# Later norms at stage changes, layer 0's context first, and weight low parts on VectorE in a two-block transformer kernel

## The chip, the core and the metric

The kernel runs on one core of a Trainium2 chip. The metric is device time of one execution in microseconds (us). Engines: TensorE (PE in the profile; its weight loads are PEld), VectorE (DVE), ScalarE (ACT), GpSimd (POOL) and SyncE (SP), which here only issues DMAs.

## The reference

Two blocks of two layers each, on 512 tokens of width 1024, all in float32. The first block also carries 256 context tokens through its layer 0.

```python
for i in range(2):                                   # first block
    u_lat = modulate(rms_norm(h_lat, g_mix[i]), sh1, sc1)    # shifts and scales: silu(c) @ ada_w[i]
    u_ctx = modulate(rms_norm(h_ctx, g_mix[i]), csh1, csc1)
    # i = 0: neighbourhood attention (16 heads) over a 8x64 grid plus context; i = 1: sliding window
    h_lat = h_lat + ga1 * y_lat                      # y = attention @ wo; layer 0: h_ctx likewise
    h_lat = h_lat + ga2 * squared_relu_mlp(
        modulate(rms_norm(h_lat, g_mlp[i]), sh2, sc2), mlp_w1[i], mlp_w2[i])
for l in range(2):                                   # second block
    hn = rmsnorm(h, pre_g)
    y = even_mixer(hn) if l == 0 else odd_mixer(hn)  # diff. attention + mLSTM; gated spatial mixing
    h = h + rmsnorm(y, post_g)
```

Width of the MLPs: 4096. The output is `h` of the 512 tokens.

## The kernel before, in words

Activations lie transposed: features on the 128 partitions, eight tiles `hl[:, k, :]` of 512 tokens (`hc` for the 256 context tokens). Each large matmul is done in parts: a float32 operand is split into a high part (fp32r, a copy on ScalarE) and a low part (the float32 value minus that copy), by `split` (lines 125 to 128), and three products are summed: hi by hi, hi by lo, lo by hi. `lin` (line 145) does it for weights as the stationary operand, first all products with the weights' high part, then those with the low part (line 152); `tok` (line 154) for tokens as the stationary operand (line 160). Weights come by `load_w` (line 132): two DMAs of half a block into `wraw`, and four splits of 128x512. Their low parts are subtracted on GpSimd unless a call names another engine. `whi` and `wlo` have two buffers, `wraw` four.

An RMS norm is `rstd` (line 259): squares on ScalarE (line 266), seven adds on VectorE (line 268), a matmul with ones that sums over the partitions (line 270; line 272 for a late last square), `Ln` and `Exp` on ScalarE. `modulate` (line 277) follows for each of the eight tiles: a product on VectorE (line 280), then the split; for odd tiles the low part is on GpSimd, for even ones on VectorE (line 289, or 128).

Stages in order of time (us of the profile): adaLN and first norms (to 60), neighbourhood attention (to 460), its output projection `project_back(0)` (to 520), `mlp(0)` (to 1098), `sliding_window` (to 1340) and `project_back(1)` (to 1375), `mlp(1)` (to 1736), the even mixer with differential attention (to 2030), mLSTM (to 2285) and its output projection (to 2347), the odd mixer (to the end).

`project_back` does the first two blocks of columns for all tokens; the last two are done token group by token group, and after each group `done` is called, which is the norm of the next stage for that group. In layer 0 the groups are all 512 tokens, then the context; in layer 1 two halves of 256. `mlp` takes eight groups of hidden features; `up(g+1)` is emitted before `down(g)`. In `up(0)` each token group has its own matmuls; in the last `down` the tokens are in halves, then the context, and `done` is called after each. `update` (line 418) adds a product times its gate to the residual, on VectorE. During `mlp(0)` the adaLN products of layer 1 are made on VectorE by `ada_vector` (lines 229 and 231), some steps at each `between()` after a weight load. `project_out` is the output projection of the second block; with `room` it calls `done(c)` after each half, which there is the post norm and the next pre norm. In the odd mixer, `value_tile` makes values of 128 tokens, with Gelu on ScalarE after the last norm's `Exp` (`issue_after`).

The order of the source gives precedence: work emitted first goes first on an engine when it can, and a scheduler at build time sets the order of each engine's queue. [...]

## Time and profile before

| | us |
|---|---|
| median of 3 runs | 2733.99 |
| lowest and highest | 2729.48, 2734.04 |
| the profiled run, its own time | 2738.25 |
| its span in the profile | 2736.4 |
| TensorE busy in it | 2603.4 |

The page's slices show TensorE busy nine tenths and more in nearly all of the 40 slices. "Busy" of TensorE counts from the start of a matmul to its modelled end; successive matmuls overlap, so the pitch of a run of matmuls is read from its length over their count. [...] In a list of waits, the instruction named after the arrow is the one that ended the idle time.

### The profile page before, as it was taken

Reading aid. Unit: us, or ns where it says so; the run is one execution under the profiler, and the core shown is the slowest. Engines: PE = TensorE matmul, PEld = TensorE weight load, DVE = VectorE, ACT = ScalarE, POOL = GpSimd, SP = SyncE. Lnnn points to the kernel's source line nnn. Section 1 sums busy time; section 2 is a strip of 40 time slices with the busy share of each in tenths; the row PEclk is TensorE's granted clock in tenths of the full one; section 3 lists DMA queues with packets and bytes.
Section 4 is the critical chain, followed back from the end, with each engine's and each line's share of the span. In section 5 each row is a group of like instructions: output and inputs, shape, how many; then the busy total and the mean of one; then the engine's idle time right before and its main releaser. Section 6 shows DMA issues by size and latency. Waiting matters only on the chain. (4 is left out here: it accounts for less than half of the span.)

```text
span 2736.4 us, 40968 instructions
## 1 busy us (share of the span) xinstructions
PE 2603.4 (95%) x15876; PEld 2201.9 (80%) x15876; DVE 1405.6 (51%) x2908; ACT 1254.8 (46%) x2664; POOL 1087.3 (40%) x932
## 2 busy tenths in 40 slices
PE   6999998999999999899999999899999999899998
PEld 4877776788888889777888888877778888898887
DVE  4667667675666567688552222544553444502024
ACT  5655555422222223588543332466654554544342
POOL 3221313333332322533254544544435555435453
PEclk9999999999999999999999999999999999999999
DMA  7211324243333342210123333322222222322321
GB/s 246 61 55 56 107 63 153 66 135 100 114 117 118 92 124 62 74 32 19 45 88 97 93 100 100 81 62 62 67 66 78 78 83 72 97 80 91 95 87 62
DMA packets 217635, 237.94 MB, mean 87 GB/s; under 512 B 9824, under 2 KB 179296, under 8 KB 217440
## 3 DMA queue, kind: packets, MB, share of 16 engines
q1 hardware_dynamic: 210464, 229.15, 27.7%
q10 hardware_dynamic: 6976, 6.17, 0.7%
q8 instruction: 125, 2.05, 0.3%
q14 instruction: 70, 0.57, 0.1%
HBM read 233.18 MB, written 2.10 MB: 86 GB/s over the span
## 5 line engine op out<-in xcount | busy, mean ns | idle before, releaser
L128 POOL TENSOR_TENSOR wlo<-wraw,whi 128x512 fp32r<-128x512 f32 x628 | 836.4, 1361 | 887.3 <-ACT whi L127 847.3
L152 PE MATMUL mm<-uhl,whi 128*128 128x512 f32 (+1 forms) x1480 | 574.3, 391 | 3.6 <-ACT whi L127 2.6
L152 PE MATMUL mm<-ull,whi 128*128 128x512 f32 (+1 forms) x1480 | 569.9, 388 | 4.3 <-POOL ull L128 2.1
L127 ACT ACTIVATE whi<-wraw 128x512 fp32r<-128x512 f32 (+1 forms) x632 | 354.0, 619 | 445.2 <-issue 276.7
L152 PE MATMUL mm<-uhl,wlo 128*128 128x512 f32 (+1 forms) x1480 | 406.3, 386 | 0.0
L152 PEld LDWEIGHTS mm<-uhl,whi 128*128 128x128 f32 x1480 | 282.0, 191 | 62.8 <-ACT whi L127 6.1
L152 PEld LDWEIGHTS mm<-ull,whi 128*128 128x128 f32 x1480 | 282.2, 191 | 56.9 <-POOL ull L128 3.7
L152 PEld LDWEIGHTS mm<-uhl,wlo 128*128 128x128 f32 x1480 | 270.2, 190 | 54.1 <-issue 2.2
L418 DVE SCALAR_TENSOR_TENSOR hl<-mm,mod,hl 128x512 f32<-128x512 f32 (+1 forms) x156 | 105.2, 679 | 226.9 <-PE mm L152 226.9
L152 PE MATMUL mm<-h1h,whi 128*128 128x512 f32 (+1 forms) x576 | 208.4, 369 | 0.0
L152 PE MATMUL mm<-h1l,whi 128*128 128x512 f32 (+1 forms) x576 | 208.1, 369 | 0.0
L152 PE MATMUL mm<-h1h,wlo 128*128 128x512 f32 (+1 forms) x576 | 161.8, 368 | 0.0
L160 PE MATMUL mm<-whi,uhl 128*128 128x256 f32 x608 | 155.0, 290 | 1.0 <-DVE t L297 0.5
L160 PE MATMUL mm<-whi,ull 128*128 128x256 f32 x608 | 152.9, 287 | 0.0
L231 DVE SCALAR_TENSOR_TENSOR aacc<-araw,csil,aacc 128x512 f32<-128x512 f32 x196 | 148.5, 811 | 2.5 <-DMA araw<-ada_w 2.4
L304 POOL TENSOR_TENSOR t<-t,t 128x512 f32<-128x512 f32 (+1 forms) x46 | 49.1, 1067 | 231.5 <-ACT t L301 132.1
L479 DVE TENSOR_TENSOR t<-mm,t 128x512 f32<-128x512 f32 (+1 forms) x96 | 53.1, 574 | 153.2 <-ACT t L474 153.1
L474 ACT ACTIVATE t<-mm 128x512 f32<-128x512 f32 (+1 forms) x100 | 47.7, 507 | 177.8 <-PE mm L152 177.8
L152 PE MATMUL mm<-ulc,whi 128*128 128x256 f32 x448 | 124.6, 286 | 1.1 <-POOL ulc L128 1.1
L152 PE MATMUL mm<-uhc,whi 128*128 128x256 f32 x448 | 124.8, 287 | 0.0
L152 PEld LDWEIGHTS mm<-h1h,whi 128*128 128x128 f32 x576 | 108.6, 188 | 19.6 <-issue 1.0
L152 PEld LDWEIGHTS mm<-h1l,whi 128*128 128x128 f32 x576 | 108.6, 189 | 18.7
(381 smaller groups left out, 5445.2 us busy)
## 6 DMA issues: line engine op xcount, KB each, us to landing
wraw<-mlp_w SPq DMA_DIRECT2D x128, 512.0 KB, 3.8
wraw<-l_w_in SPq DMA_DIRECT2D x88, 512.0 KB, 3.7
araw<-ada_w SPq DMA_DIRECT2D x112, 256.0 KB, 3.0
wraw<-l_w_out SPq DMA_DIRECT2D x32, 512.0 KB, 3.5
wraw<-ada_w SPq DMA_DIRECT2D x24, 512.0 KB, 4.2
wraw<-l_w_in SPq DMA_DIRECT2D x48, 256.0 KB, 3.3
wraw<-na_wqkv SPq DMA_DIRECT2D x32, 256.0 KB, 3.8
wraw<-swa_wqkv SPq DMA_DIRECT2D x12, 512.0 KB, 3.6
```

Source lines behind the costliest of these rows:

```text
L127: nc.scalar.activation(out=hi, in_=src, func=AF.Copy)
L128: lo_eng.tensor_tensor(out=lo, in0=src, in1=hi.bitcast(F32), op=ALU.subtract)
L152: nc.tensor.matmul(out=o[0], lhsT=a[:, i, ms], rhs=o[j][:, i, :], start=(start and n_ == 0), stop=(stop and n_ == len(terms) - 1))
L160: nc.tensor.matmul(out=ps, lhsT=x[:, i, :], rhs=w[:, i, :], start=(n_ == 0), stop=(n_ == len(terms) - 1))
L231: nc.vector.scalar_tensor_tensor(out=acc[v], in0=raw, scalar=x, in1=acc[v], op0=ALU.mult, op1=ALU.add)
L304: nc.gpsimd.tensor_tensor(out=q, in0=q, in1=r, op=ALU.mult)
L418: nc.vector.scalar_tensor_tensor(out=o, in0=ps, scalar=mod[i][:, 8 * which + m, v:v + 1], in1=h, op0=ALU.mult, op1=ALU.add)
L474: nc.scalar.activation(out=a, in_=p, func=AF.Relu)
L479: nc.vector.tensor_tensor(out=q, in0=p, in1=a, op=ALU.mult)
```

## The change

- `pending` is a list of postponed norms, and `flush(n)` emits them. Where `done` was called, it is now put on the list. `flush` is called halfway through the next token group: in `project_back` after block 2 of the columns, in `up(0)` before the third tile, in the last `down` before the fifth, in the sliding window between a group's keys and values, in the even mixer after the first half's queries and keys. In `project_out` and the odd mixer the post norm and the pre norm are flushed one by one.
- In layer 0 the context is the first group of `project_back` and of `up(0)`, and the 512 tokens follow in two halves. In `up(0)` (both layers) both weight blocks are loaded first, and all four tiles of a group follow one another.
- The low part of a weight is subtracted on VectorE, except within the head loops of the two attentions (`scr["lo"]` is GpSimd there, and VectorE again for the last pair of heads of the neighbourhood attention).
- In the odd mixer the first half's values of the first four blocks are summed two tiles to a bank, before the Gelu of any of them.

```diff
...
     upool = ctx.enter_context(tc.tile_pool(name="upool", bufs=1))
-    scr = {}
+    scr = {"lo": nc.vector}
...
                 y = slice(s.start + x.start, s.start + x.stop)
-                split(hi[:, y, :], lo[:, y, :], raw[:, x], lo_eng or nc.gpsimd)
+                split(hi[:, y, :], lo[:, y, :], raw[:, x], lo_eng or scr["lo"])
         return hi, lo
...
+    pending = []
+    def flush(n=9):
+        for _ in range(min(n, len(pending))):
+            pending.pop(0)()
...
-        def segments(ul, uc, halves=False):
+        def segments(ul, uc, halves=False, ctx_first=False):
             lat = [(0, hlat, c, parts(ul, c)) for c in HALF] if halves else [(0, hlat, LAT, ul)]
-            return lat + ([(1, hctx, CTX, uc)] if uc is not None else [])
-        def project_back(i, w, x, halves, done, room=None, ws=()):
+            c = [(1, hctx, CTX, uc)] if uc is not None else []
+            return c + lat if ctx_first else lat + c
+        def project_back(i, w, x, done, room=None, ws=()):
             whole = segments(*x)
-            split_ = segments(*x, halves=halves)
+            split_ = segments(*x, halves=True, ctx_first=True)
             ws = [*ws, None, None, None, None]
...
                         update(i, 2, 2 * b + m, v, h(2 * b + m)[:, c], p)
-                done(v, h, c)
+                    if b == 2:
+                        flush()
+                pending.append(lambda v=v, h=h, c=c: done(v, h, c))
...
                     hid = hidden()
-                    for b in range(2):
+                    def load(b):
                         w = load_w([(0, 256, w1[:, 512 * g + 256 * b:512 * g + 256 * b + 256])], KD, 256)
                         between()
-                        sg = segments(*x, halves=halves and g == 0)
-                        groups = [[s] for s in sg] if g == 0 else [sg]
-                        for grp in groups:
-                            for m in range(2):
-                                j = 2 * b + m
-                                o = [(mm_tile()[:, :c.stop - c.start], xx) for _, _, c, xx in grp]
-                                lin([(p, *xx) for p, xx in o], w, slice(128 * m, 128 * m + 128))
-                                for (p, _), (v, _, c, _) in zip(o, grp):
-                                    act(p, hid[v][0][:, j, c], hid[v][1][:, j, c], i == 0 and g == 7 and v == 0)
+                        return w
+                    def tile_of(w, j, grp):
+                        o = [(mm_tile()[:, :c.stop - c.start], xx) for _, _, c, xx in grp]
+                        lin([(p, *xx) for p, xx in o], w, slice(128 * (j % 2), 128 * (j % 2) + 128))
+                        for (p, _), (v, _, c, _) in zip(o, grp):
+                            act(p, hid[v][0][:, j, c], hid[v][1][:, j, c], i == 0 and g == 7 and v == 0)
+                    if g == 0:
+                        ws = [load(b) for b in range(2)]
+                        for s in segments(*x, halves=True, ctx_first=True):
+                            for j in range(4):
+                                if j == 2:
+                                    flush()
+                                tile_of(ws[j // 2], j, [s])
+                    else:
+                        for b in range(2):
+                            w = load(b)
+                            for j in (2 * b, 2 * b + 1):
+                                tile_of(w, j, segments(*x))
                     return hid
...
                         for m in range(8):
+                            if last and m == 4:
+                                flush()
                             o = [(mm_tile()[:, :c.stop - c.start], xx) for _, _, c, xx in grp]
...
                             for v, h, c, _ in grp:
-                                done(v, h, c)
+                                pending.append(lambda v=v, h=h, c=c: done(v, h, c))
...
                 banks(mm="01", AD="2", NS="7", S="34", PT="5", ST="6")
+                scr["lo"] = nc.gpsimd
                 for hp in range(8):
...
                     if hp == 7:
+                        scr["lo"] = nc.vector
                         oh = (u_lat(), u_ctx())
...
-                project_back(0, A["na_wo"], oh, False, norm_after(0, "mlp", u), room, ws)
+                project_back(0, A["na_wo"], oh, norm_after(0, "mlp", u), room, ws)
             return u
+            if 1 not in u:
+                u[1] = u_ctx()
             ul, uc = u[0], u[1]
...
                         stack_k(kh[m], s, t)
+                    flush()
                     for t in range(n // 128):
...
                     split(oh[0][:, t, :], oh[1][:, t, :], pv, nc.vector)
+                scr["lo"] = nc.vector
                 banks(mm="0124", NS="7")
                 u = {}
-                project_back(1, A["swa_wo"], (oh, None), True, norm_after(1, "mlp", u))
+                project_back(1, A["swa_wo"], (oh, None), norm_after(1, "mlp", u))
             return u
...
                     block_out(b, c)
-                done(c)
+                    if b % 2 == 0:
+                        flush(1)
+                pending.extend(done(c))
             return
...
                 qk_proj(0, w0, HALF[x:x + 1])
+                flush()
                 v_proj(0, range(2 * x, 2 * x + 2))
...
         def done(c):
-            post_norm(yacc, vec("post0"), c)
-            norm(0, hlat, c)
+            return [lambda: post_norm(yacc, vec("post0"), c), lambda: norm(0, hlat, c)]
...
-        def value_tile(b, wv, t):
-            ps = mm_tile()[:, :256]
+        def value_mm(ps, wv, t):
             tok(ps, wv, parts(u, slice(128 * t, 128 * t + 128)))
+        def value_out(ps, b, t):
             o = vt[:, t, 256 * b:256 * b + 256]
+        def value_tile(b, wv, t):
+            ps = mm_tile()[:, :256]
+            value_mm(ps, wv, t)
+            value_out(ps, b, t)
...
         wv += [value_w(2 + j, (y[:, :, 0:256], y[:, :, 256:512]), nc.vector) for j, y in enumerate(y_tiles())]
-        with tc.issue_after(last_exp.ins):
+        early = []
+        for b in range(4):
+            ps = mm_tile()
+            for t in range(2):
+                value_mm(ps[:, 256 * t:256 * t + 256], wv[b], t)
+            early.append(ps)
+            if b % 2 == 0:
+                flush(1)
+        with tc.issue_after(scr["rstd"].ins):
             for b in range(4):
                 for t in range(2):
-                    value_tile(b, wv[b], t)
+                    value_out(early[b][:, 256 * t:256 * t + 256], b, t)
         for b in range(4):
...
```

## Rows read from the trace of the kernel before

**Rows 1.** The page, part 1: busy us (share of the span) xinstructions by engine
```profile
PE 2603.4 (95%) x15876; PEld 2201.9 (80%) x15876; DVE 1405.6 (51%) x2908; ACT 1254.8 (46%) x2664; POOL 1087.3 (40%) x932
```
**Rows 2.** TensorE's waits, whole span: who waited for whom, us in total, times, longest us
```profile
PE NS L270 <- DVE acc L268: 38.3, 10, 16.5
...
PE PT L1043 <- DVE p L1040: 8.6, 8, 2.0
PE NS L270 <- DVE pr L1007: 7.1, 1, 7.1
...
PE CU L1188 <- DVE kw L1186: 4.9, 3, 1.7
...
PE mm L152 <- DVE yl L128: 2.2, 1, 2.2
...
PE mm L160 <- POOL wlo L128: 1.2, 2, 0.7
```
**Rows 3.** Windows: stretch, length; busy of PE, PEld, DVE, ACT, POOL; PEclk; DMA share, GB/s
```profile
507.00:560.00 53.00, 43.23 (x249) 36.31 (x248) 47.24 (x67) 26.72 (x54) 22.37 (x16) 0.90 0.32 100
560.00:1060.00 500.00, 497.66 (x2993) 429.66 (x2992) 306.76 (x463) 119.78 (x239) 155.59 (x112) 1.00 0.37 112
1060.00:1121.00 61.00, 54.86 (x429) 52.33 (x428) 44.56 (x88) 34.78 (x83) 28.48 (x32) 0.97 0.18 57
...
1345.00:1392.00 47.00, 41.06 (x291) 38.55 (x290) 29.89 (x50) 23.78 (x57) 22.99 (x21) 0.96 0.30 87
...
1711.00:1752.00 41.00, 33.17 (x243) 32.03 (x242) 30.27 (x50) 18.68 (x46) 21.82 (x22) 0.88 0.31 84
...
2300.00:2374.00 74.00, 65.78 (x503) 64.38 (x502) 54.46 (x97) 32.91 (x85) 29.95 (x28) 0.93 0.27 84
```
**Rows 4.** Windows again, over ten stretches of low clock: one, and the sum
```profile
1741.00:1745.30 4.30, 0.00 (x0) 0.00 (x0) 4.20 (x3) 1.15 (x2) 3.44 (x3) 0.50 0.57 148
...
sum 37.60, PE 29.54 PEld 27.14 DVE 26.62 ACT 18.94 POOL 13.42; mean PE 2.95 PEld 2.71 DVE 2.66 ACT 1.89 POOL 1.34
```
**Rows 5.** Timelines, three stretches: start us, us, engine line op xcount [idle before <-releaser]
```profile
533.15 0.41 DVE L268 TENSOR_TENSOR acc<-acc,t 128x256 f32<-128x256 f32 x1
...
534.61 1.22 PE L270 MATMUL NS<-acc,ones 128*128 128x256 f32 x2 [5.15 <-DVE acc L268]
...
1725.18 0.70 PE L270 MATMUL NS<-acc,ones 128*128 128x256 f32 x2 [0.48 <-DVE acc L268]
...
1740.74 3.70 POOL L128 TENSOR_TENSOR wlo<-wraw,whi 128x512 fp32r<-128x512 f32 x3
1740.87 4.38 DVE L268 TENSOR_TENSOR acc<-acc,t 128x256 f32<-128x256 f32 x2
1745.31 1.22 PE L270 MATMUL NS<-acc,ones 128*128 128x256 f32 x2 [7.09 <-DVE pr L1007]
1745.97 0.78 PE L152 MATMUL mm<-uhl,wlo 128*128 128x256 f32 x1
```
**Rows 6.** The chain that ended last: start us, us, what (256 columns, then 512)
```profile
2364.26 79.54 PE mm L160 x666
2443.80 21.79 PE mm L152 x96
```
**Rows 7.** Timeline of VectorE after 534.61: last low part of that norm
```profile
542.23 0.47 DVE L289 SCALAR_TENSOR_TENSOR ulc<-t,mod,uhc 128x256 fp32r<-128x256 f32 x1
```
**Rows 8.** Groups of instructions: busy us, mean ns; or duration ns min/median/max
```profile
L128 POOL TENSOR_TENSOR wlo<-wraw,whi 128x512 fp32r<-128x512 f32 x624 | 833.6, 1365 | 884.3 <-ACT whi L127 847.3 <-PE mm L152 17.3 <-issue 10.9
L128 POOL TENSOR_TENSOR wlo<-wraw,whi x628: 727/1295/1868, 54.2 to 2703.8; 128x512 fp32r<-128x512 f32 x156, 128x256 fp32r<-128x256 f32 x1
L128 DVE TENSOR_TENSOR wlo<-wraw,whi x4: 684/686/693, 37.5 to 40.1; 128x512 fp32r<-128x512 f32 x4
L418 DVE SCALAR_TENSOR_TENSOR hl<-mm,mod,hl 128x256 f32<-128x256 f32 x40 | 18.5, 477 | 8.3 <-PE mm L152 8.3
```
**Rows 9.** Line 1227 on VectorE: duration ns min/median/max, first and last start
```profile
L1227 DVE SCALAR_TENSOR_TENSOR nctionType.Sigmoid<-nctionType.Sigmoid,vecs,t x8: 804/1702/1759, 2142.9 to 2290.8; 128x512 f32<-128x512 f32 x8
```

More of the change, by code (lines that the diff above doesn't have):

```diff
@@ L463, in mlp @@
         def mlp(i, with_ctx, u, done, between=lambda: None):
-            halves = not with_ctx
             x = (u[0], u[1] if with_ctx else None)
@@ L820, in sliding_window @@
                 banks(mm="0", NS="7", SL="12", SC="3", PT="45", ST="6")
+                scr["lo"] = nc.gpsimd
                 for t in range(8):
@@ L1250, in even, with odd @@
         return nu[0]
-    def odd(bp, yp, u, last_exp):
+    def odd(bp, yp, u):
         wi = A["l1_w_in"]
@@ L1345 @@
                 with tc.tile_pool(name="odd", bufs=1) as bp, tc.tile_pool(name="oddy", bufs=1) as yp:
-                    odd(bp, yp, u, scr["rstd"])
+                    odd(bp, yp, u)
     if stop < 5:
```

## The prediction

> **What bounds the kernel now.** I read the page's busy times first: TensorE is busy 95% of the span, the others about half or less [rows 1]. So the time is TensorE's work, plus its idle time, plus what it loses at the lower clock. Next comes the list of TensorE's waits [rows 2]. The largest is line 270, the ones-matmul that sums the squares of an RMS norm over the partitions, waiting for VectorE's adds (line 268): 38.3 us, and 7.1 us more put down to `pr`, a VectorE instruction just behind those adds. Of these 45.4 us the longest, 16.5, lies at the start of the kernel, which the change doesn't touch. The other 28.9 us (a short one at the very end among them) lie at five stage changes: neighbourhood attention to MLP 0, MLP 0 to sliding window, sliding window to MLP 1, MLP 1 to the even mixer, even to odd mixer.
>
> The table of windows [rows 3] gives length and TensorE's busy time at these five: 53-43.23, 61-54.86, 47-41.06, 41-33.17 and 74-65.78, together 37.9 us idle, of which 28.9 are the waits above and 9.0 are others. The granted clock is below 1 in each; in the 500 us of MLP 0 between them it is 1.00, with 2.3 us idle. [...]
>
> Why do the waits occur? The matmul at 1745.31 stood still for 7.09 us, and what follows it is the next stage's first tile (line 152, `uhl`): all of TensorE's later work queued behind one norm [rows 5]. What it waited for is VectorE's adds, and these are stretched: one 128x256 add takes 0.41 us alone, but two of them take 4.38 us while GpSimd runs three weight subtractions (3.70 us, line 128) in the same place. So at a stage change VectorE stands still while GpSimd subtracts, and TensorE stands still for VectorE.
>
> **The change part by part.** *Norms later.* A norm's instructions are now emitted after half of the next token group. Half a group of 256 tokens is 48 matmuls; 666 of that width took 79.54 us [rows 6], 0.119 us each, so 5.7 us. The two longest of the waits were 7.09 and 5.15 us [rows 5]: 5.7 us of other matmuls in front covers all but 1.4 us of the longer. I count 28.9-1.4 = 27.5 us gained. Where a gap remains the clock can still fall: of the 14.8 us I leave 4, about a quarter; 10.8 gained.
>
> The price: the next stage's input comes later. From a norm's matmul at 534.61 to the last of its low parts, 542.23+0.47, is 8.1 us [rows 5, 7]. Where the normed half is the very next thing read (MLP 1, the even and the odd mixer), 5.7 us of matmuls are left when its norm's matmul is issued, and 16 matmuls of 0.119 us (1.9 us) of the next tile go by before the last part is needed: 7.6 against 8.1. That is no margin. VectorE's load says the same. In the 23 us (192 matmuls) in which both halves of a norm must pass there are eight updates of 0.477 us, seven adds of 0.41, twelve instructions of 0.47 for the modulation, eight of about 0.41 for four tiles' activations, and now eight weight subtractions of 0.686 [rows 5, 7, 8]: 3.8+2.9+5.6+3.3+5.5 = 21.1 us. A new wait there lies between nothing and the old 7; I take 2 us at each of the three, 6 in sum, near the case just computed. At the other two changes the context's group lies between, 11.4 us more, and I take none, though at the first VectorE was busy 47.24 of 53 us [rows 3], with the adaLN products of line 231 in the same queue.
>
> *Context first, tokens in halves* (layer 0's output projection and first MLP group). 96+96 matmuls of 512 columns become twice as many of 256. 96 of 512 took 21.79 us, 0.227 each [rows 6]; two of 256 take 0.239. 192 x 0.012 = 2.4 us lost, on TensorE and so on the path. The vector work cut in two (products, adds, low parts) adds some 4 us on VectorE beside it, hidden as long as VectorE is ahead there; if it isn't, it is 4 us.
>
> *Low parts on VectorE.* Ten loads inside the neighbourhood loop and three in the sliding window's stay on GpSimd; of the others some 147 loads of four subtractions, 588 in all, move. GpSimd loses 588 x 1.365 = 803 us, VectorE gains 588 x 0.686 = 403 us [rows 8] and goes from 51% of the span to some 61%, the stretching gone. GpSimd's time was hardly on the path itself: TensorE waited 1.2 us for it [rows 2]. In MLP 0, the heaviest long stretch, VectorE goes from 307 to at most 307+128 x 0.686 = 395 of 500 us [rows 3]. So the subtractions cost nothing as long as they aren't queued behind a late instruction. At the changes they replace the stretch by work of a like size (three are 2.1 us, against 4.38-0.82 = 3.6 us of stretch), so I count nothing there. The gain lies in the mLSTM and in differential attention. Line 1227 takes 1.70 us as a rule and 0.80 at best, twice in a row [rows 9], and three state updates wait 4.9 us behind such pairs [rows 2]; I take 4. The wait of 2.2 us for the last head's low part, behind line 1227 and GpSimd's queue: 3, with some low clock that follows it, between 0 and 4. The 8.6 us of line 1043 wait for VectorE's scaled probabilities [rows 2]: 3, between 0 and 8.6, because VectorE now has subtractions in the same place. Together 10 us.
>
> [...]
>
> *Value tiles of the odd mixer* are summed two to a bank before the norm's last exponential. No matmul is added; it lets the flushes stand between them and is counted in the 27.5.
>
> **The sum.** 27.5+10.8-6-2.4+10 = 39.9 us off the profiled span of 2736.4, 2696.5. The profiled run took 2738.25, 1.85 more than its span and 4.3 above the median of the three runs, 2733.99. On the median's scale: 2733.99-39.9 = 2694.
>
> **The rivals.** First, *the wait moves instead of going.* Late norms make the next stage's first matmuls wait in all five places, 4 us each, and the clock falls as before: 27.5-20+10-2.4 = 15.1 gained, 2719. For it: 7.6 against 8.1 above, and VectorE nearly full at the first change. Against: a norm of the same trace in the middle of a group, at 1725.18, cost 0.48 us [rows 5].
>
> Second, *the queue's order doesn't follow the source*, and the norms stand where they stood, or VectorE's new subtractions eat all that the stretching cost. Then only 10-2.4 remain: 2726. For it: one norm matmul in the trace (1745.31) stands inside a tile of the next stage and not where the source has it, so the order in a queue is not the source's.
>
> Third, *slower: low parts late.* A subtraction queued on VectorE behind an update that itself waits for TensorE comes late, and TensorE waits for the weights just split. One subtraction late per load is 147 x 0.686 = 101 us. It outweighs the 39.9 when it befalls two loads in five; at one in two the time is 2694+51 = 2745. For it: VectorE's queue is full of instructions that wait for TensorE, the updates of line 418 above all. Against: a load has two buffers, and GpSimd, at twice the time per subtraction, was late by 1.2 us in total. [...]
>
> Fourth, *all of it*: no new waits, the clock never down, half of the other 9.0 us gone, and nearly all of line 1043's: 6+4+4.5+5.5 = 20 more, 2674.
>
> **How the numbers follow.** Forecast 0.52; wait moved 0.20; order unchanged 0.12; low parts late 0.08; all of it 0.08. About 0.2% (5.5 us) is what a measurement of this kernel can tell from no change. Faster: 0.52+0.20+0.08 and a third of the second rival, 0.84; within 0.2%: the rest of that, 0.08; slower 0.08. Range: from 2671, just under the fourth case, to 2722, where the first rival ends with 3 us for GpSimd's delays.
>
> **What would show it.** Right: line 270's waits at the five changes fall from 28.9 us to a few, with few stretches below full clock; GpSimd's busy time is near 285 us; no 128x256 add takes 1 us or more; 192 more matmuls run on line 152. The first rival shows as waits of lines 152 and 160 for `uhl` or `ull` right after a change. The second shows as line 270 with its old waits. The third shows as line 152 waiting for `wlo` from VectorE all through the MLPs. The prediction is wrong if line 270 no longer waits and TensorE's idle time stays.

## The result, and the profile after

The changed kernel takes 2689.72 us (median of 5 runs, 2686.89 to 2692.43), 0.9844 of the kernel before (95% interval 0.983 to 0.9859): 42.6 us less. The kernel before, run beside it, has a median of 2732.59 us over 5 runs. The profiled run took 2692.43 us, its span is 2690.3.

The first lines are of the page (busy us, share, instructions), then of the list of TensorE's waits (us in total, times, longest), of the groups of instructions (busy us, mean ns), and of the adds' durations (min/median/max in ns). All are of the changed kernel but the last line, which shows the same adds in the kernel before. The changed kernel's lines 129, 153, 161, 269, 271, 300, 426, 1079 and 1224 are 128, 152, 160, 268, 270, 299, 418, 1043 and 1188 of before.

```profile
PE 2596.4 (97%) x16070; PEld 2207.2 (82%) x16070; DVE 1622.2 (60%) x3527; ACT 1252.6 (47%) x2691; POOL 316.7 (12%) x348
```
```profile
PE NS L271 <- DVE acc L269: 22.9, 8, 15.0
PE NS L300 <- ACT t L297: 12.1, 9, 3.6
...
PE mm L161 <- ACT yh L128: 2.0, 1, 2.0
...
PE mm L161 <- ACT whi L128: 1.2, 1, 1.2
...
PE mm L153 <- DVE hl L426: 1.0, 1, 1.0
```
```profile
L129 DVE TENSOR_TENSOR wlo<-wraw,whi 128x512 fp32r<-128x512 f32 x576 | 383.9, 707 | 376.2 <-ACT whi L128 239.0 <-PE mm L153 79.6 <-PE mm L161 56.5
...
L129 POOL TENSOR_TENSOR wlo<-wraw,whi 128x512 fp32r<-128x512 f32 x52 | 71.6, 1400 | 53.9 <-ACT whi L128 41.3 <-PE mm L153 12.0 <-DVE nm L314 0.5
```
```profile
L269 DVE TENSOR_TENSOR acc<-acc,t x122: 407/425/962, 9.3 to 2677.4; 128x256 f32<-128x256 f32 x115, 128x512 f32<-128x512 f32 x7
```
```profile
L268 DVE TENSOR_TENSOR acc<-acc,t x115: 405/426/3851, 9.0 to 2723.5; 128x256 f32<-128x256 f32 x101, 128x512 f32<-128x512 f32 x14
```

Apart from the 15.0 us at the start, 7.9 us are left of line 271's waits, against 28.9 [rows 2]. The longest add falls from 3851 ns to 962. Line 1079's waits for probabilities and line 1224's for `kw` [rows 2] are no longer on the list. TensorE's idle time falls from 133 to 94 us, and 192 more matmuls run on line 153 (9912 against 9720). So the signs that the prediction asked for are there, two of them in part: GpSimd is busy 316.7 us where 285 were expected, and 20.4 us at the lower clock (a granted clock of 0.50, where 1.00 is the full one) are left at the changes (37.6 in [rows 4]). The signs don't tell which part of the change did it, and the experiments give another answer than the sum did.

The table is worked out from the traces. Each kernel's span is cut at the same instructions: the first and last transposes of each attention loop, the first and last matmuls that read an MLP's hidden low and high parts, the mLSTM's numerators, the odd mixer's first mixing matmul. Lengths in us; "five changes" are the stretches between one stage's loop and the next (longer than the windows of [rows 3]). "Late norms alone" has the new token order too; of the last two columns the first has the old token order and the second the new one. Each column is one trace; the start, where the third last column and "changed" run the same source, differs by 1.9 us between them, so a difference of that size in one stage says little.

| stage | before | changed | low parts alone | late norms alone | changed, prompt norms | prompt, more on VectorE | late, more on VectorE |
|---|---|---|---|---|---|---|---|
| start and neighbourhood loop | 459.0 | 450.4 | 450.5 | 455.9 | 448.5 | 440.5 | 441.2 |
| five changes | 564.3 | 544.5 | 525.7 | 566.5 | 528.1 | 513.3 | 531.6 |
| both MLPs | 799.8 | 797.6 | 797.1 | 800.6 | 797.7 | 795.3 | 796.4 |
| sliding-window loop | 162.3 | 164.9 | 163.5 | 162.0 | 163.5 | 162.8 | 161.4 |
| differential attention | 229.9 | 219.3 | 220.4 | 229.7 | 220.4 | 220.2 | 220.1 |
| to the mLSTM, and mLSTM | 250.0 | 242.4 | 242.4 | 249.8 | 242.3 | 242.4 | 242.4 |
| rest of the odd mixer | 271.0 | 271.0 | 271.0 | 271.3 | 271.0 | 271.0 | 271.0 |

At the five changes the changed kernel gained 19.8 us, where the sum had 29.9 (27.5+10.8-6-2.4). Elsewhere it gained 26.3, where the sum had 10.

### The profile page after: what moved, and what is told of

Its sections match the earlier page's. It is cut to its first block, busy times and chain, and to the rows that moved or that the text cites. A ratio compares the mean times of both kernels' runs of the same rounds, so it can differ in the third digit from the quotient of the medians.

```text
span 2690.3 us, 41389 instructions
## 1 busy us (share of the span) xinstructions
PE 2596.4 (97%) x16070; PEld 2207.2 (82%) x16070; DVE 1622.2 (60%) x3527; ACT 1252.6 (47%) x2691; POOL 316.7 (12%) x348
## 4 chain that ended last, share of the span: by engine, by line
PE 81%; DVE 10%; ACT 7%; issue 1%; DMA 1%; POOL 0%; SPq 0%; DVEq 0%; POOLq 0%; ACTq 0%
PE mm L153 60%; PE mm L161 7%; DVE t L281 1%; PE ST L701 1%; PE PT L680 1%; PE ST L864 1%; PE PT L847 1%; PE NS L300 1%; PE S L347 1%; DVE wlo L129 1%; ACT qx L327 1%; PE PO L1083 1%; ACT qx L333 1%; PE S L348 1%; PE AD L183 1%
## 5 line engine op out<-in xcount | busy, mean ns | idle before, releaser
L129 DVE TENSOR_TENSOR wlo<-wraw,whi 128x512 fp32r<-128x512 f32 (+1 forms) x580 | 385.5, 705 | 379.0 <-ACT whi L128 239.0
L153 PEld LDWEIGHTS mm<-uhl,whi 128*128 128x128 f32 x1528 | 288.2, 189 | 61.4 <-DVE t L298 4.4
L153 PEld LDWEIGHTS mm<-ull,whi 128*128 128x128 f32 x1528 | 288.5, 189 | 57.2 <-POOL ull L129 5.3
L129 POOL TENSOR_TENSOR ull<-t,uhl 128x256 fp32r<-128x256 f32 (+1 forms) x44 | 41.3, 944 | 1028.6 <-ACT uhl L128 1028.3
L232 DVE SCALAR_TENSOR_TENSOR aacc<-araw,csil,aacc 128x512 f32<-128x512 f32 x196 | 136.2, 751 | 0.4 <-DMA araw<-ada_w 0.4
L161 PEld LDWEIGHTS mm<-whi,uhl 128*128 128x128 f32 x608 | 116.8, 192 | 4.4 <-ACT whi L128 1.6
```

What stands on the lines that cost most here:

```text
L129: lo_eng.tensor_tensor(out=lo, in0=src, in1=hi.bitcast(F32), op=ALU.subtract)
L153: nc.tensor.matmul(out=o[0], lhsT=a[:, i, ms], rhs=o[j][:, i, :], start=(start and n_ == 0), stop=(stop and n_ == len(terms) - 1))
L161: nc.tensor.matmul(out=ps, lhsT=x[:, i, :], rhs=w[:, i, :], start=(n_ == 0), stop=(n_ == len(terms) - 1))
L232: nc.vector.scalar_tensor_tensor(out=acc[v], in0=raw, scalar=x, in1=acc[v], op0=ALU.mult, op1=ALU.add)
```

## The experiments

The first four split the change and test the stretch; four more say where it sits; the last four carry it further. Every ratio is to the kernel before, with its 95% interval.

**Low parts alone** (e1_low_parts_only).

```diff
 (kernel before)
-    scr = {}
+    scr = {"lo": nc.vector}      # nc.gpsimd inside the two attention loops
...
-                split(hi[:, y, :], lo[:, y, :], raw[:, x], lo_eng or nc.gpsimd)
+                split(hi[:, y, :], lo[:, y, :], raw[:, x], lo_eng or scr["lo"])
```

> The kernel before, with one edit: the weights' low parts are subtracted on VectorE instead of GpSimd, but for the loads inside the two attention loops, as in the changed kernel. Norms and token order stay as before. Theory A (two gains of like size): TensorE's interior waits go, since VectorE is no longer held up by GpSimd's subtractions: differential attention about 9 us shorter, mLSTM about 6, start and neighbourhood about 5, and at the five changes the norm's adds are no longer stretched, so line 270's 28.9 us shrink to about 20; the norm's own length stays there. About 20 to 28 us below the kernel before (0.7 to 1.0%). Rival B (all of it is the stretch of the adds): the waits of line 270 go with the stretch alone, about 40 us below. Rival C (the later norms do it all, the prediction's own weighting): 10 us below, the mLSTM and line 1043 only.

Measured: 2672.8 us, ratio 0.978 (0.9767 to 0.9794), 60 us below the kernel before, and 17 below the changed kernel. Its list of TensorE's waits, and line 268's durations:

```profile
PE NS L270 <- DVE acc L268: 22.3, 9, 15.0
PE NS L299 <- ACT t L296: 9.3, 10, 1.7
```
```profile
L268 DVE TENSOR_TENSOR acc<-acc,t x115: 405/424/957, 9.3 to 2657.7; 128x256 f32<-128x256 f32 x101, 128x512 f32<-128x512 f32 x14
```

In the source norms stand where they stood, and yet line 270 waits 7.3 us outside the start instead of 28.9; the five changes are 38.6 us shorter. Theory A's 20 to 28 and rival C's 10 fall. Rival B has the mechanism (the waits were the stretch of the adds) and too small a number, 40; the interior gains come on top. A rival that no run separates: the build sets TensorE's queue anew, and in it the norm's matmul stands 13, 10, 25 and 12 places later at the last four changes. At 0.119 us a matmul [rows 6] that is some 7 us of cover, an estimate. At the first change the matmul has the same place in both queues, and its wait still falls from 5.15 to 0.97 us.

**Late norms alone** (e2_norms_only).

```diff
 (changed kernel)
-    scr = {"lo": nc.vector}
+    scr = {"lo": nc.gpsimd}      # and so wherever it is set later
```

> The changed kernel with the weights' low parts back on GpSimd everywhere; norms half a group later, context first and tokens in halves as in the changed kernel. Theory A: the five changes keep most of their gain, since 5.7 us of matmuls stand in front of each norm, but the stretched adds and the later low parts eat some of it: 15 to 22 us below the kernel before. Rival B: next to nothing below it (within 5 us), since the norm is still held up by GpSimd's subtractions. Rival C: about 30 us below it, as the prediction's sum has it without the low parts.

Measured: 2736.84 us, ratio 1.0011 (1.0002 to 1.002): 0.5 to 5.5 us slower than the kernel before. Rival B holds, rival C (the prediction's weighting) is out. Its waits, first over the span, then from 1725 to 1790 us (MLP 1 to the even mixer) and from 1370 to 1430 (to MLP 1), and the durations of its adds:

```profile
PE NS L271 <- DVE acc L269: 27.9, 8, 15.7
...
PE PT L1079 <- DVE p L1076: 7.5, 8, 2.0
...
PE mm L238 <- issue: 5.3, 1, 5.3
...
PE CU L1224 <- DVE kw L1222: 4.9, 3, 1.6
```
```profile
PE mm L161 <- ACT whi L128: 4.1, 1, 4.1
PE NS L1044 <- DVE pr L1042: 2.6, 1, 2.6
```
```profile
PE mm L153 <- POOL ull L129: 2.8, 5, 1.2
```
```profile
L269 DVE TENSOR_TENSOR acc<-acc,t x122: 407/426/4371, 9.0 to 2722.7; 128x256 f32<-128x256 f32 x115, 128x512 f32<-128x512 f32 x7
```

The adds are as stretched as before (4371 ns at most). The delay did cover norms: line 271 waits 12.2 us outside the start, against 28.9. But TensorE's idle time at the five changes, added up from the traces, is 41.1 us against 44.0: of the 16.7 us covered, 13.8 came back. Among it are waits of the next stage's matmuls for high parts of weights queued behind the norm on ScalarE (4.1, none there before), for the norm's own low parts (2.8, 0.3 before), and of an adaLN product (5.3, 3.3 before). Most of the wait moved instead of going.

**Layer 0's tokens whole and in the old order** (e3_whole_tokens).

```diff
 (changed kernel)
-            split_ = segments(*x, halves=True, ctx_first=True)
+            split_ = segments(*x, halves=x[1] is None)
...
-                        for s in segments(*x, halves=True, ctx_first=True):
+                        for s in segments(*x, halves=not with_ctx):
```

> The changed kernel with layer 0's token order undone: in its output projection and in the first group of its MLP the 512 latent tokens go in one piece and before the context; norms stay late, low parts stay on VectorE. Theory A (192 matmuls at 0.012 us, and a stage in which VectorE has more, smaller instructions): 2.4 us less of matmuls, 192 matmuls fewer, but a wait of up to 5 us where the MLP's first tile reads all 512 tokens right after their norm: from 2 us shorter to 3 us longer than the changed kernel. Rival: the split tokens are what makes the first change cheap, and without them its 10 us of waits and low clock come back: 8 us longer or more.

Measured: 2691.63 us, ratio 0.9847 (0.9834 to 0.986), not to be told from the changed kernel, inside theory A's range. In its first change TensorE is busy 1.5 us less and idle 4.1 us more than in the changed kernel: the waits for the norm and for the normed input (from 450 to 600 us) eat what the wider matmuls save.

```profile
PE NS L271 <- DVE acc L269: 2.6, 1, 2.6
PE mm L153 <- ACT uhc L289: 2.2, 1, 2.2
PE mm L153 <- POOL ull L129: 2.0, 3, 1.3
```

**Spare subtractions on GpSimd** (e4_idle_copies). They compute nothing that is used.

```diff
 (changed kernel, after each subtraction that moved)
+                if (lo_eng or scr["lo"]) is nc.vector:
+                    h = hi[:, y, :].bitcast(F32)
+                    nc.gpsimd.tensor_tensor(out=junk[...], in0=h, in1=h, op=ALU.subtract)
```

> The changed kernel, and on GpSimd, for each subtraction that moved to VectorE, one subtraction of the same size whose result nobody reads (high part minus itself into a spare tile). Nothing waits for GpSimd that didn't before, apart from the spare work standing in its queue; the computation is the same. Theory A (VectorE is held up by GpSimd's reading and writing of SBUF): VectorE's instructions are stretched again, 100 to 150 us in sum over the span, and of the 43.6 us gained 15 to 30 are given back. Rival D (what counted was that the low part came late from a slow engine, 1.365 us against 0.686): the stretch may return, yet the time stays within 5 us of the changed kernel.

Measured: 2780.57 us, ratio 1.0172 (1.0158 to 1.0186): 91 us above the changed kernel, 47 above the kernel before. GpSimd is busy 1082.2 us, as before (1087.3, [rows 1]), and no instruction reads these results. TensorE, VectorE and ScalarE execute the same instructions as in the changed kernel, in the same order but for a few places, so queue order has no part in the 91 us. The groups of instructions (busy us, mean ns), then one group of the changed kernel, whose line 426 is line 430 here, then two of the waits with spare subtractions (line 275 is line 271 of the changed kernel):

```profile
L148 POOL TENSOR_TENSOR junk<-whi 128x512 f32<-128x512 f32 x576 | 741.7, 1288 | 926.5 <-ACT whi L129 890.8 <-DVE rl L845 3.4
...
L130 DVE TENSOR_TENSOR wlo<-wraw,whi 128x512 fp32r<-128x512 f32 x576 | 625.8, 1126 | 256.0 <-ACT whi L129 194.1 <-PE mm L157 60.8 <-issue 0.8
...
L130 DVE TENSOR_TENSOR h1l<-t,h1h 128x512 fp32r<-128x512 f32 x56 | 46.3, 826 | 12.8 <-ACT h1h L129 12.4
...
L430 DVE SCALAR_TENSOR_TENSOR hl<-mm,mod,hl 128x512 f32<-128x512 f32 x112 | 82.4, 746 | 117.8 <-PE mm L157 117.5
```
```profile
L426 DVE SCALAR_TENSOR_TENSOR hl<-mm,mod,hl 128x512 f32<-128x512 f32 x112 | 83.9, 750 | 171.5 <-PE mm L153 171.2
```
```profile
PE NS L275 <- DVE acc L273: 35.8, 10, 15.3
...
PE mm L165 <- ACT whi L129: 4.8, 1, 4.8
```

The subtraction on VectorE goes from 707 to 1126 ns, 241 us in sum: theory A's direction, with three times the upper end of its price. The moved subtractions, which follow the same high parts as the spare ones, take most of the stretch. Line 275 waits 20.5 us outside the start instead of 7.9, though the adds read no low part of a weight. Rival D, which wanted the time unchanged, falls; but since the low parts were late here too (1126 ns), the run doesn't separate stretch from lateness for the loads. Nor does it hold that nothing waits for the spare work: ScalarE's next high part waits 18 times, 223.2 us in all, until GpSimd has read `whi`. What reaches TensorE of this is little: its waits for `whi` and `wlo` are 9.2 us here and 3.0 in the changed kernel.

**Prompt norms in the changed kernel** (e6_prompt_norms).

```diff
 (changed kernel, the first pair of lines twice)
-                pending.append(lambda v=v, h=h, c=c: done(v, h, c))
+                done(v, h, c)
...
-                pending.extend(done(c))
+                for f in done(c):
+                    f()
```

> The changed kernel with one part undone: each norm is emitted as soon as its tokens are finished, as in the kernel before. Context first, tokens in halves, the two-to-a-bank value tiles and the low parts on VectorE stay. Known so far: low parts alone 2673, the changed kernel 2690. Theory E (the delay itself costs: norms that come half a group later leave their input late for the next stage's first tile, and the split tokens cost some 4.4 us of matmuls): 2675 to 2681, that is the low parts alone plus the split tokens. Rival F (the split and reordered tokens, or the value tiles, cost all 17 us): 2687 to 2692, as the changed kernel.

Measured: 2674.67 us, ratio 0.9788 (0.9774 to 0.9801). Just under the lower end of theory E. The delay costs 15 us (0.9844 against 0.9788). All else that came with it, split tokens, context first and value tiles, is 2 us above the low parts alone, within the intervals. At the first change by itself, where the split tokens are, it is 6.5 us (143.3 against 136.8, one trace each), of which 3.4 go to 6.8 us at the lower clock, 0.50 (the granted clock of the whole run is 0.996, with the low parts alone 0.998).

**Low parts only beside the changes** (e5_low_parts_at_changes): 41 of some 147 loads.

```diff
 (low parts alone)
-    scr = {"lo": nc.vector}
+    scr = {"lo": nc.gpsimd}
...
+                    scr["lo"] = nc.vector if g < 2 else nc.gpsimd            # MLP, up
+                    scr["lo"] = nc.vector if g == 0 or g > 5 else nc.gpsimd  # MLP, down
+            scr["lo"] = nc.gpsimd   # from differential attention on, nc.vector from the last projection to the odd mixer's sixth load
```

> The kernel before, with VectorE subtracting the low parts only of the some 41 loads that run next to the five stage changes (output projections, the first two and last groups of each MLP, the first loads of sliding window, even and odd mixer); all other loads stay on GpSimd, norms stay where they were. Theory G (the waits at the changes were VectorE held up by GpSimd's subtractions in the same microseconds): the five changes gain as with all low parts moved, 33 to 39 us, and differential attention, the mLSTM and the start gain nothing: 2694 to 2702. Rival H (it is the relief over the whole kernel, a backlog of VectorE that the MLPs build up): well under half of it, 2715 or more.

Measured: 2690.82 us, ratio 0.9845 (0.9832 to 0.9858). Theory G, a little beyond its range: 42 of the 60 us come from these loads. The five changes take 527.0 us (525.7 with all low parts moved), differential attention 230.9, as before. Theory G missed the start and neighbourhood loop, which it had at no gain: 450.9 us, 8.1 shorter, 5.2 of it in the last two pairs of heads, beside which the first of the 41 loads run. The interior waits stand as they stood:

```profile
PE PT L1049 <- DVE p L1046: 8.6, 8, 2.0
...
PE CU L1195 <- DVE kw L1193: 4.9, 3, 1.6
```

**The loads inside the attention loops too** (e7_all_weights).

```diff
 (low parts alone, twice)
-                scr["lo"] = nc.gpsimd
+                scr["lo"] = nc.vector
```

> Low parts on VectorE as in the kernel with them alone (2673), now for the 13 loads inside the two attention loops too: 52 subtractions more on VectorE (36 us more work, some 18 us less stretch), GpSimd 71 us less. Theory I (a VectorE that isn't held up has room): 0 to 6 us shorter. Rival J (in these loops VectorE's chain of softmax steps is on the path, and a subtraction in front of it costs its 0.69 us): 5 to 20 us longer, with the waits of the transposes for `p` up.

Measured: 2658.83 us, ratio 0.9732 (0.9718 to 0.9745), 13 us below the low parts alone; more than theory I had, and rival J's waits don't come. Start and neighbourhood take 439.6 us instead of 450.5. Line 651, one SBUF operand scaled by a column, in the kernel before and here:

```profile
L651 DVE TENSOR_SCALAR p<-p,rl x64: 471/486/1522, 88.8 to 451.8; 128x512 f32<-128x512 f32 x64
```
```profile
L651 DVE TENSOR_SCALAR p<-p,rl x64: 470/482/733, 83.3 to 434.0; 128x512 f32<-128x512 f32 x64
```

**The norms' odd low parts too** (e8_norm_parts).

```diff
 (low parts alone)
-            split(uh, ul, t, nc.gpsimd if k % 2 else nc.vector)
+            split(uh, ul, t, nc.vector)
...
-                split(uh, ul, t, nc.gpsimd)
+                split(uh, ul, t, nc.vector)
```

> Low parts on VectorE as in the kernel with them alone (2673), and the norms' odd low parts as well, 52 subtractions of 128x256 or 128x512 that GpSimd still does (50 us there). Theory K (GpSimd's last work in a norm still holds VectorE up, 15 to 18 us of stretch): 1 to 5 us shorter. Rival L (inside a norm VectorE is the longer queue, and each odd part adds 0.41 us to it): 2 to 8 us longer, as waits of the next stage's first tile for `ull` from VectorE.

Measured: 2657.74 us, ratio 0.9721 (0.9708 to 0.9734), 16 us below the low parts alone, three times theory K's upper end. Here splitting a norm's work over two engines was slower than one engine doing all: the waits for GpSimd's `ull` and `ulc` are gone and line 270 waits 4.8 us outside the start, nearly all on the way to the odd mixer and at the end. How much of this is VectorE relieved and how much order isn't shown: six of the norms' matmuls, line 270's, stand 7 to 25 places later in TensorE's queue than with the low parts alone, 79 in all (some 10 us at 0.119 us for 256 columns and 0.227 for 512, an estimate).

**Both** (e9_weights_and_norms), **and the same with late norms** (e10_late_norms_free): the two edits above, on the low parts alone and on the changed kernel.

> The kernel before with all weights' low parts and the norms' odd low parts on VectorE; norms at their old place. The two steps, one by one, brought 2673 to 2659 and to 2658. Theory R (they remove the stretch at different places, the attention loops and the five changes): the two gains add, 2641 to 2648. Rival S (VectorE, at some 61%, takes no more): 2653 or more.

> The changed kernel (late norms, context first, tokens in halves) with all weights' low parts and the norms' odd low parts on VectorE. Compared with the same at prompt norms, which runs beside it. Theory P (the 15 us that late norms cost were again stretch: they push VectorE's chains of the next stage beside GpSimd's remaining subtractions, as in sliding window, where line 308 took 1.47 us instead of 0.41): the delay is now worth between a gain of 3 and a loss of 4 us, and the split tokens cost some 4 us: 0 to 8 us above the prompt one. Rival Q (late norms leave the next stage's input late, whoever subtracts): 14 us above it or more.

Measured: 2646.94 us, ratio 0.9688 (0.9674 to 0.9702): theory R, the gains add but for 4 us (25 of 29). With late norms 2666.0 us, ratio 0.976 (0.9746 to 0.9774): 19 us more, so rival Q, not theory P. The 19 us include the new token order; less the 2 to 5 us for that, the delay costs 14 to 17 us, as much as where GpSimd still subtracts (15). VectorE's stretch, as defined in the last section, is 48 us in both. The change from MLP 1 to the even mixer, as waits of TensorE, prompt (1677 to 1728 us) and late (1690 to 1745), and VectorE's queue in the late one:

```profile
PE S L346 <- DVE nm L313: 0.5, 1, 0.5
PE NS L1013 <- ACT rstd L273: 0.2, 1, 0.2
```
```profile
PE mm L153 <- DVE hl L426: 1.5, 1, 1.5
PE mm L161 <- ACT whi L128: 0.6, 1, 0.6
```
```profile
1691.81 1.27 DVE L281 SCALAR_TENSOR_TENSOR t<-hl,vecs,rstd 128x256 f32<-128x256 f32 x3
...
1696.20 0.88 DVE L281 SCALAR_TENSOR_TENSOR t<-hl,vecs,rstd 128x256 f32<-128x256 f32 x2
1696.99 0.48 DVE L426 SCALAR_TENSOR_TENSOR hl<-mm,mod,hl 128x256 f32<-128x256 f32 x1
...
1698.05 1.26 DVE L426 SCALAR_TENSOR_TENSOR hl<-mm,mod,hl 128x256 f32<-128x256 f32 x3
```

From 1691.81 to 1696.99 VectorE works on the norm alone, while the updates of the last tiles (line 426) stand behind it, and by the profile TensorE's next tile waits for such an update. With prompt norms TensorE waits 0.7 us there; that the following half group of matmuls covers the same instructions is read from the order of the source. Of the 19 us, the first change takes 8.8 (6.4 of it longer matmul time: 1.7 through 3.4 us at the lower clock, 0.50, the rest put down to the split tokens), the fourth 4.5 (2.3 idle, the rest matmuls at a mean granted clock of 0.96 instead of 1.00); the rest is spread, 1.7 at most in one stage.

At sliding window theory P was right, though: there the delay costs 5.7 us in the changed kernel (72.8 against 67.1 with prompt norms) and 1.7 here (67.1 against 65.4). In the changed kernel the late norm of the context moves the keys' head norms beside the subtractions that GpSimd still does for the attention loop's loads. VectorE's queue there, ScalarE's and the matmul that waited, and GpSimd's (timelines of the changed kernel; line 297 stands behind line 341 in ScalarE's queue):

```profile
1131.43 1.47 DVE L308 TENSOR_TENSOR t<-t,t 128x256 f32<-128x256 f32 x1
...
1136.66 1.37 DVE L308 TENSOR_TENSOR t<-t,t 128x256 f32<-128x256 f32 x1
1138.06 0.85 ACT L341 ACTIVATE ky<-t 64x256 fp32r<-64x256 f32 x2 [2.48 <-DVE t L308]
...
1139.59 2.07 PE L300 MATMUL NS<-t,blk 128*128 128x512 f32 x2 [3.65 <-ACT t L297]
```
```profile
1131.33 2.72 POOL L129 TENSOR_TENSOR wlo<-wraw,whi 128x512 fp32r<-128x512 f32 x2 [0.65 <-ACT whi L128]
...
1135.00 2.74 POOL L129 TENSOR_TENSOR wlo<-wraw,whi 128x512 fp32r<-128x512 f32 x2
```

**GpSimd's other two-operand work on VectorE** (e11_gpsimd_free).

```diff
 (as before it: rotary products, post norm's odd additions, gates, the mixers' low parts)
-        nc.gpsimd.tensor_tensor(...)
+        nc.vector.tensor_tensor(...)
```

> As the kernel with weights and norms on VectorE, and GpSimd's other two-operand work (products of the rotary embedding, half of the post norm's additions, gates, low parts of the mixers' outputs, about 190 us there) on VectorE too; GpSimd keeps small copies and memsets. Theory: what is left of the stretch (some 35 us) goes, VectorE gains about 95 us of work: between 2 us longer and 8 us shorter. Rival J again (head norms and gates are chains on VectorE in front of TensorE's matmuls, and the second queue ran beside them): 3 to 15 us longer.

Measured: 2634.23 us, ratio 0.9645 (0.9632 to 0.9659): the fastest of all, 13 us below the one with weights and norms on VectorE (the theory had 8 at most) and 55 below the changed kernel (0.9844 to 0.9645). Rival J falls in the loops where it should have shown: differential attention takes 213.5 us instead of 220.2. The page, and the weights' subtraction in the groups of instructions:

```profile
PE 2569.2 (98%) x15876; PEld 2188.5 (83%) x15876; DVE 1660.3 (63%) x3736; ACT 1256.9 (48%) x2667; POOL 37.1 (1%) x104
```
```profile
L128 DVE TENSOR_TENSOR wlo<-wraw,whi 128x512 fp32r<-128x512 f32 x628 | 406.9, 684 | 321.5 <-ACT whi L127 148.4 <-PE mm L152 111.2 <-PE mm L160 60.6
```

VectorE has taken over GpSimd's two-operand arithmetic and is busy only 255 us more than before (1405.6, [rows 1]), for 1050 us less on GpSimd; its subtraction of weights is at 684 ns.

**Spare copies instead of spare subtractions** (e12_idle_one_input).

```diff
 (spare subtractions)
-                    nc.gpsimd.tensor_tensor(out=junk[...], in0=h, in1=h, op=ALU.subtract)
+                    nc.gpsimd.tensor_copy(out=junk[...], in_=h)
```

> The changed kernel, and on GpSimd one plain copy of the high part into a spare tile, 128x512 as before, in place of the spare subtraction that cost 91 us over the changed kernel. Theory M (any work of GpSimd that reads SBUF holds VectorE up, for as long as it lasts): the price goes by the copies' busy time; if a copy takes 0.6 to 1.0 us against the subtraction's 1.28, 40 to 75 us over the changed kernel. Rival N (only GpSimd's instructions with two operands from SBUF do): within 10 us of the changed kernel.

Measured: 2715.74 us, ratio 0.994 (0.9927 to 0.9953), 26 us above the changed kernel: between the two, and neither's number. The groups:

```profile
L148 POOL COPY junk<-whi 128x512 f32<-128x512 f32 x576 | 456.5, 793 | 1102.7 <-ACT whi L129 1074.0 <-DVE rl L845 3.4 <-POOL junk L148 0.6
...
L130 DVE TENSOR_TENSOR wlo<-wraw,whi 128x512 fp32r<-128x512 f32 x576 | 484.4, 880 | 330.1 <-ACT whi L129 260.4 <-PE mm L157 69.5
```

The spare copies, which read one operand, hold VectorE up too: its subtraction takes 880 ns instead of 707, 100 us in sum against 241 with spare subtractions. The price, 29% of the other's, goes more nearly by the stretch (41%) than by GpSimd's busy time on spare work (62%), and by neither in proportion. ScalarE waits for the spare copies too, 148.7 us, as it did for the spare subtractions.

## Why the prediction was right in its number and wrong in its reasons

The forecast was 2694, the result 2690. Three terms of the sum were wrong and cancelled, by luck: measured, the low parts gave 60 us, the delay took 15 and the rest 2, together the 43 that came out. Two readings were off without moving the sum: the second longest wait of line 270 at a change was 5.36 us (at 2329.9), not 5.15, and the 4.38 us of "two adds" are one add of 3.85 and one of 0.42.

*Norms later: the failing step.* The sum gave the delay 27.5+10.8-6 = 32.3 us. Without the low parts, late norms and the new token order are worth -3 us; on top of the low parts the delay by itself is worth -15. The prediction saw the cause itself (adds stretched while GpSimd subtracts [rows 5]) and then treated the wait as one of order, to be covered by 5.7 us of matmuls. The cover worked in part (28.9 to 12.2 us with late norms alone), but most of what was covered came back, as the first rival said, in waits of the next stage; the prediction gave that 0.20 and put 2 us in each of three places. The wait for `ull` at MLP 1 is 2.8 us; at the change to the even mixer it was not the normed input that came late but what stood in VectorE's and ScalarE's queues behind the norm, updates and high parts of weights. That each queue the norm was moved past holds other work for TensorE was missing from the rival. No run shows the clock's 14.8 us, and 10.8 of them gained, as such: the traces show TensorE busy at a granted clock of 0.50 for 29.54 us before [rows 4] and for 18.3 us at the changes in the changed kernel. Half of each, 14.8 and 9.1 us, is an estimate of what is lost; with the low parts alone it is 1.7. So this gain didn't come from the delay either.

*Low parts at the changes: the other half of it.* "At the changes they replace the stretch by work of a like size ... so I count nothing there." With all low parts moved the changes are 38.6 us shorter. Three subtractions on VectorE are indeed 2.1 us. But at the change to the even mixer the norm's seven adds, with five subtractions among them, take 7.1 us from first to last with low parts alone; before, with none among them, 9.4. And 41 loads at the changes gave 42 us with nothing else altered in the source. The step compared three subtractions with the stretch of two adds, where it should have summed the stretch of all that stands in front of line 270.

*Low parts in the interior: right places, under-sized.* The mLSTM with its last head: 4 and 3 expected; that stretch gained 7.6 us. Line 1043: 3 expected, at most 8.6; differential attention gained 9.5 to 10.6, the whole of the upper bound and more, and its waits came back exactly when its loads went back to GpSimd (8.6). Nothing was counted for the start and the neighbourhood loop: 8.5. That the interior waits fell with the low parts alone is shown; how much of it is stretch and how much queue order isn't.

*Split tokens*: 2.4 expected. With prompt norms everything that came with them costs 2 us over the low parts alone, inside the intervals; the 2.4 is neither confirmed nor refuted.

*GpSimd and VectorE*: 285 and 61% of the span expected, 316.7 us and 60% measured; GpSimd's 52 remaining subtractions of weights take 1400 ns (1365 before, [rows 8]). The range's upper end has 3 us for GpSimd's delays, a term that no run shows; the traces show the norms' odd low parts on GpSimd at 911 ns in the changed kernel and 810 before (`ull`, 128x256).

*Low parts late*, the third rival: lines 152 and 160 wait 2.9 us in all for VectorE's `wlo` in the kernel with low parts alone. It didn't decide. Where line 426's updates stood late in VectorE's queue, behind 5.2 us of instructions (1691.81 to 1696.99, above), it was the late norm that stood in front of them and not the weights. *The queue's order*, the second rival, had line 270 keep its old waits, and it didn't.

*Which of VectorE's work was stretched.* With 600 spare subtractions on GpSimd, `h1l` (128x512), whose operands all lie in SBUF, took 826 ns and 689 in the changed kernel; line 430, which reads a matmul's sum, took 746 and 750 there. Line 651, with one operand and a column, took up to 1522 ns before and 733 at most once the loops' loads were moved. The sum has no term for the norms' odd low parts: taken off GpSimd they gave 16 us (with some queue order in it, above), and GpSimd's other two-operand work, taken off last, gave 13 more.

*The signs.* Line 270's waits, the adds' longest, the clock, GpSimd's time: all went the way that was named, and all do so with the low parts alone too. A sign that both parts of a change would leave can't tell which of them works.

## What to carry to other kernels

When an engine's instruction is several times longer than its usual (here an add of 3.85 us instead of 0.41), look for what runs beside it before moving it elsewhere in the order: here the neighbour was worth some 60 us (a little of it perhaps queue order) and the place -15. Work given to GpSimd "because it is free" wasn't free here: 600 spare subtractions cost 91 us, as many spare copies 26, and all of its two-operand work, moved, left VectorE only 255 us busier for 1050 us less on GpSimd. So compare the sum of both engines, and split a change into its parts on the chip, since a right total says nothing about them.

## What the runs showed of the hardware

- A VectorE add that takes 0.41 us alone took 3.85 us (1740.87 to 1744.72) under three GpSimd subtractions in a row, which ended at 1744.44 [rows 5]: here one add was held up through several of GpSimd's instructions. The add before it, beside a GpSimd memset (1740.25 to 1740.77), took its usual 0.415 us.
- The 128x512 subtraction takes 684 ns on VectorE with GpSimd nearly idle (the fastest kernel), a mean of 1126 in the kernel with GpSimd's spare ones, and 1365 on GpSimd itself [rows 8]; spare results that nobody reads cost 91 us over 600 instructions.
- Stretch and time, where stretch is the sum over VectorE's instructions of what each takes above the 10th percentile of its group: 219 us before, 80 with low parts alone, 48 with all weights and norms, 20 with GpSimd nearly idle, at 2733, 2673, 2647 and 2634 us. That is 0.4 to 0.8 us of time for each us of stretch, though TensorE, busy 95 to 98% of the span, is the engine that sets the end. Put back by spare work it cost less: 0.2 (copies, 209 us against the changed kernel's 92) to 0.3 (subtractions, 409). Late norms alone leave it at 209 us, and late norms at 48 us of stretch still cost 19 us: stretch is not the only cause of a wait here.
